# Grouped-query attention of a fused layer step: maxima of two heads in one pair of matmuls, tiles of keys two by two, and other engines for copies and sums

## The chip, the cores and the metric

The kernel runs on one core of a Trainium2 chip. Its metric is the device time of one execution in microseconds (us). The profile gives for the core the busy time of its engines: TensorE (PE, with its weight loads as PEld), VectorE (DVE), ScalarE (ACT), GpSimd (POOL) and the queue of SyncE (SP), which issues most DMAs.

## The reference

One layer of a hybrid backbone for 256 context tokens and 2048 latent tokens: three mixers (differential attention, grouped-query attention, a state-space scan) share an input and an output projection, and a feed-forward layer follows. The change is in the grouped-query attention of the latent tokens. It has four query heads of width 64, two for each of two key heads, and 2560 keys (2048 latent, 512 cached):

```python
qg = q.reshape(b, t, GQA_KV_HEADS, GQA_Q_HEADS // GQA_KV_HEADS, GQA_HD)
s = jnp.einsum('bqkgd,bskd->bkgqs', qb, k).astype(jnp.float32) * scale
p = jax.nn.softmax(s, axis=-1).astype(v.dtype)
return jnp.einsum('bkgqs,bskd->bqkgd', p, v)
```

## The kernel before, in words

The function `attention` (line 842) first does the differential heads, 64 steps and 7 more that drain its pipeline, and then the grouped heads. These are cut into eight units (line 933): a key head `j` and a stretch of 512 queries, both query heads of the group together. Queries and keys are kept as a rounded part in the float32r format and the remainder, in stacks: `qa` holds for each head 64 partitions of the rounded part and 64 of the remainder, `qb[0:64]` the rounded part again, and its partition 64 takes the negated maximum of each query. `gk[j][:, 0]` holds the rounded keys twice, in partitions 0-63 and 64-127; `gk[j][0:65, 1]` their remainder and a row of ones.

A unit has two parts. `maxima` (line 945) finds for each query the maximum over all keys of an approximate score, `qa` times `gk[j][:, 0]`: for each head and each 128 queries five matmuls of 512 keys, each reduced by VectorE out of its bank into `gmx` (lines 959 and 960); then a reduction to `nm` (962), transposes (967) and two copies of a row into `qb` (968). `weighted` (line 971) goes over 20 tiles of 128 keys: four matmuls give the scores of both heads less the maximum (981 and 982, product of two parts each), ScalarE takes the exponential of the two banks at once into `ge` (984), and two tiles later the values are accumulated, the two heads in 64 columns of the array each (990; an f32 matmul is two instructions in the profile). The sum of the exponentials is kept in `ga`, by VectorE for tiles 1 and 3 of every five and by GpSimd for the others (998 and 1000). `unit_tail` (1006) adds the two sums (1009), turns the output (1013), sums over the partitions by matmuls with ones (1020) and divides (1023, 1025).

The order is written out by hand with generators. While `weighted` of unit `ui` runs, each of its 44 steps takes one step of `maxima` of unit `ui + 1`, so that a maximum's matmul stands between scores and values; every second step takes one of the tails, of the attention of the context tokens (`contexts`, units 1 to 3) and of the loads and splits of the output weights (`OutProj.weights`, from unit 4 on, lines 1398 and 1399). Every engine works its instructions in this order. The queries of the next unit are loaded at the start of a unit (`group_queries`, line 936, on SP's queue), into buffers that come free with the last scores of the unit before. The maxima of unit 0 run with wider pieces of 1024 keys (`wide`) in the seven steps that drain the differential heads.

Of the eight PSUM banks the scores have two buffers of two banks (`ps_s`), the single tiles two buffers of one bank (`ps_t`), the outputs two banks.

## Time and profile before

| | |
|---|---|
| three runs, median (range) | 3765.62 us (3758.86 to 3769.51) |
| profiled execution: its own time, its span | 3772.03 us, 3770.2 us |
| TensorE matmuls busy, instructions | 3586.9 us (95%), 20178 |
| VectorE | 2490.2 us (66%), 4092 |
| ScalarE | 1787.6 us (47%), 2890 |
| GpSimd | 1797.8 us (48%), 1448 |

A busy share is a mean over stages with different limits. The matmuls of TensorE overlap and their ends are modelled, so that the distance of two starts says what one costs, and the duration how long its result takes. An idle time is put down to what ended it. Stretches are in us from the start of the span; the grouped heads lie from about 1481 to 1957 us.

### The profile page before, as it was taken

The numbers are of one execution on the slowest core, as the hardware profiler recorded it, in microseconds if no ns is written. First come the engines' busy times: TensorE is split into PE (matmuls) and PEld (weight loads), VectorE is DVE, ScalarE is ACT, GpSimd is POOL, SyncE is SP. The second block draws the span as 40 slices with busy tenths as digits, with TensorE's granted clock in tenths as the row PEclk, the third lists the DMA queues.
The fourth block names the chain that finished last, engine by engine and source line by source line (L and its number), as shares of the span: only waits on it lengthen the run. The fifth ranks groups of instructions, "written<-read, shape, count | busy, mean of one in ns | idle before, by whom it ended". The sixth has DMA issues, their size and how long they took to land.

```text
span 3770.2 us, 53905 instructions
## 1 busy us (share of the span) xinstructions
PE 3586.9 (95%) x20178; PEld 2884.0 (76%) x20178; DVE 2490.2 (66%) x4092; ACT 1787.6 (47%) x2890; POOL 1797.8 (48%) x1448
## 2 busy tenths in 40 slices
PE   6999899988999999999999989999999999999998
PEld 4888699984555555454458879999999999888886
DVE  3666766658889888767746776656556555465476
ACT  3555545546888885444334443334334333333232
POOL 3334356645788886445544567774233232011011
PEclk8999899998999999999999999999999999999999
DMA  5111244345311103001014656665454444645464
GB/s 199 49 46 46 76 126 124 119 130 164 97 34 42 36 22 83 14 26 48 23 62 165 209 190 216 213 216 182 153 186 164 160 154 163 231 160 175 153 217 156
DMA packets 265797, 473.65 MB, mean 126 GB/s; under 512 B 43480, under 2 KB 165752, under 8 KB 260928
## 3 DMA queue, kind: packets, MB, share of 16 engines
q1 hardware_dynamic: 247584, 456.72, 36.7%
q10 hardware_dynamic: 17232, 11.09, 1.1%
q8 instruction: 160, 2.62, 0.3%
q0 software_dynamic: 720, 2.38, 0.2%
q14 instruction: 101, 0.83, 0.1%
HBM read 345.72 MB, written 124.40 MB: 125 GB/s over the span
## 4 chain that ended last, share of the span: by engine, by line
PE 75%; DVE 9%; POOL 6%; issue 4%; DMA 3%; ACT 2%; SPq 0%; POOLq 0%; DVEq 0%; ACTq 0%
PE f L1685 6%; PE f L1684 6%; PE f L1683 6%; PE fy L1960 5%; PE fy L1962 5%; PE fy L1961 5%; PE ps L1174 4%; PE po L1234 4%; PE gpo L990 4%; PE px L225 3%; PE pt L1223 3%; PE gm L959 3%; PE gs L981 2%; PE gs L982 2%; PE opo L1447 2%
## 5 line engine op out<-in xcount | busy, mean ns | idle before, releaser
L1179 DVE TENSOR_SCALAR_CACHE_REDUCE e<-ps 128x1024 f32<-128x1024 f32 (+1 forms) x384 | 392.9, 1040 | 68.5 <-PE ps L1174 67.2
L1190 ACT ACTIVATE e<-e,nb 128x2560 f32<-128x2560 f32 x128 | 311.0, 2430 | 41.0 <-DVE nb L1184 40.9
L1960 PE MATMUL fy<-fp 128*128 128x512 f32 x792 | 308.7, 390 | 0.6 <-DVE fu L1823 0.6
L1962 PE MATMUL fy<-fp 128*128 128x512 f32 x792 | 308.7, 390 | 0.0
L1961 PE MATMUL fy<-fp 128*128 128x512 f32 x792 | 308.4, 389 | 0.0
L1212 POOL TENSOR_TENSOR e<-e,e 128x512 f32<-128x512 f32 x254 | 296.5, 1167 | 21.2
L1924 DVE TENSOR_TENSOR fp<-fo,fp 128x1536 fp32r<-128x1536 f32 (+1 forms) x110 | 208.7, 1911 | 140.5 <-ACT fp L1923 118.0
L960 DVE TENSOR_REDUCE gmx<-gm 128x1 f32<-128x512 f32 (+1 forms) x304 | 214.2, 715 | 120.0 <-PE gm L959 116.8
L1823 POOL TENSOR_TENSOR ft<-fu,fa 128x384 f32<-128x384 f32 x66 | 104.2, 1578 | 390.8 <-DVE fu L1823 342.8
L1991 POOL TENSOR_TENSOR fr<-fr,ln2b 128x1024 f32<-128x1024 f32 x17 | 54.0, 3178 | 490.6 <-DMA fo<-h_d 294.6
L1174 PE MATMUL ps<-dk,dq 96*128 96x512 f32 x640 | 244.9, 466 | 29.8 <-DVE e L1179 18.1
L1000 POOL TENSOR_TENSOR gag<-gag,ge 128x1024 f32<-128x1024 f32 x80 | 208.4, 2605 | 125.7 <-ACT ge L984 124.4
L984 ACT ACTIVATE ge<-gs 128x1024 f32<-128x1024 f32 x160 | 163.7, 1024 | 217.7 <-PE gs L982 215.3
L1923 ACT ACTIVATE fp<-fo 128x1536 fp32r<-128x1536 f32 (+1 forms) x110 | 157.2, 1442 | 195.1 <-PE fy L1962 163.8
L1211 POOL TENSOR_SCALAR e<-e,c 128x512 f32<-128x512 f32 x254 | 180.7, 711 | 115.2 <-DVE c L1203 104.9
L1174 PEld LDWEIGHTS ps<-dk,dq 96*128 96x128 f32 x640 | 101.0, 198 | 156.8 <-issue 72.1
L1224 ACT ACTIVATE wT<-pt 128x512 f32<-128x512 f32 x320 | 178.7, 591 | 67.8 <-PE pt L1223 67.1
L1234 PE MATMUL po<-wT,vl 128*64 128x256 f32 x1280 | 204.5, 407 | 0.0
L1223 PEld LDWEIGHTS pt<-cst,e 128*128 128x128 f32 x1280 | 160.7, 142 | 56.5 <-POOL e L1212 12.5
L1223 PE MATMUL pt<-cst,e 128*128 128x128 f32 x1280 | 197.1, 276 | 4.8 <-POOL e L1212 3.2
L225 PE MATMUL px<-xhTrue,wx 128*128 128x260 f32 (+2 forms) x864 | 182.1, 303 | 16.5 <-DVE l L374 7.0
L1685 PE MATMUL f<-fxt,wc 128*128 128x384 f32 x528 | 179.1, 339 | 2.6 <-DVE wc L1791 2.6
(454 smaller groups left out, 10613.0 us busy)
## 6 DMA issues: line engine op xcount, KB each, us to landing
fo<-in_wfo SPq DMA_DIRECT2D x110, 512.0 KB, 4.2
wq<-in_wfi SPq DMA_DIRECT2D x88, 512.0 KB, 3.7
wq<-ws_d SPq DMA_DIRECT2D x88, 512.0 KB, 4.2
h_d<-h SPq DMA_DIRECT2D x66, 384.0 KB, 3.0
wada<-in_w_ada SPq DMA_DIRECT2D x24, 1024.0 KB, 6.9
ws_d<-wq SPq DMA_DIRECT2D x44, 512.0 KB, 2.6
fo<-h_d SPq DMA_DIRECT2D x66, 256.0 KB, 4.1
fr<-x2T_d SPq DMA_DIRECT2D x20, 768.0 KB, 7.6
```

The source lines that it names most:

```text
L225: PE.matmul(out, l, r, start=(i == 0), stop=(i == n - 1))
L1174: PE.matmul(ps[:, 512 * c:512 * c + 512], Q[0:96, m, qs], K[0:96, m, k0:k0 + 512], start=True, stop=True)
L1179: V.tensor_scalar(self.e[m][:, k0:k0 + w], ps[:, c:c + w], dscale, -3.4e38, ALU.mult, ALU.max, accum_out=mx[:, m, seen[m]:seen[m] + 1])
L1190: S.activation(self.e[m], self.e[m], AF.Exp, bias=self.nb[:, m:m + 1], accum_out=self.l[:, m:m + 1])
L1212: G.tensor_tensor(e0[:, a:b], e0[:, a:b], e1[:, a:b], ALU.add)
L1223: PE.transpose(pt[:, k], self.e[0][:, 128 * (4 * g + k):128 * (4 * g + k) + 128], ident)
L1234: PE.matmul(po[64 * e:64 * e + 64], hd.v[:, k + e], self.wT[:, k + e], start=(k == 0), stop=(k == NKT - 2))
L1683: PE.matmul(o, w[:, 0, c, cs], x[:, 0, k], start=(k == 0), stop=False)
L1685: PE.matmul(o, w[:, 1, c, cs], x[:, 0, k], start=False, stop=(k == 3))
L1960: PE.matmul(o, x[:, 0, ts_], x[:, 0, hs], start=(f == 0), stop=False)
L1961: PE.matmul(o, x[:, 0, ts_], x[:, 1, hs], start=False, stop=False)
L1962: PE.matmul(o, x[:, 1, ts_], x[:, 0, hs], start=False, stop=(f == NF - 1))
```

## The change

The maxima are formed from the rounded parts alone: `qb` gets the second head's rounded part in partitions 64-127, and the matmuls of the two heads go to the two halves of the array's rows, into two banks. Unit 0 uses the wide buffers and one reduction for both heads; the other units take two single banks, VectorE reduces the first, ScalarE copies the second to SBUF and VectorE reduces the copy. `weighted` takes two tiles per turn: scores of two tiles, a step, values of the two tiles before, a step, 21 steps in all; the first two tiles' scores start with the matmuls that don't need the maxima. VectorE keeps the sum of every fourth tile, GpSimd of the others, each addition in two halves of 512 columns; GpSimd also adds the two sums. One row of maxima is copied by ScalarE. Every step takes a step of the side work, the tail has three steps more, the output weights have one buffer (a tag that another tile of the pool used) and three more steps between load and split.

```diff
@@ -940,65 +940,93 @@
                       gp[0].tile([128, 2, 512], F32R, name=f"q{a}{ui}", tag=f"q{a}") for a in "ab"]
             load(qa, stk_d[8 + 2 * j:10 + 2 * j, :, t0:t0 + 512].rearrange("r p t -> p r t"))
             load(qb[0:64], stk_d[8 + 2 * j:10 + 2 * j, 0:64, t0:t0 + 512].rearrange("r p t -> p r t"))
+            load(qb[64:128, 0], stk_d[9 + 2 * j, 0:64, t0:t0 + 512])
             gqs[ui] = qa, qb
 
-        def maxima(ui, wide=False):
+        def maxima(ui, sp=None):
+
+
             j, u = units[ui]
-            qa, qb = gqs[ui]
+            qb = gqs[ui][1]
             nm = nms[ui % 2]
             mx = c1.tile([128, 8, 5], F32, name=f"gmx{ui}", tag="gmx", bufs=2)
-            for r in range(2):
-                for q in range(4):
-                    ql = qa[:, r, 128 * q:128 * q + 128]
-                    pieces = range(0, KEYS, 1024 if wide else 512)
-                    for i, c in enumerate(pieces):
-                        w = min(KEYS - c, pieces.step)
-                        ps = (ps_s if wide else ps_t).tile([128, pieces.step], F32, name=f"gm{ui}_{r}{q}{c}",
-                                                           tag="s" if wide else "t")
-                        for e in range(0, w, 512):
-                            PE.matmul(ps[:, e:e + 512], ql, gk[j][:, 0, c + e:c + e + 512], start=True, stop=True)
-                        V.tensor_reduce(mx[:, 4 * r + q, i:i + 1], ps[:, 0:w], AX.X, ALU.max)
-                        yield
-            V.tensor_reduce(nm[:, :, 64], mx[:, :, 0:len(pieces)], AX.X, ALU.max, negate=True)
+            for q in range(4):
+                for i in range(5):
+                    nm_ = f"gm{ui}_{q}{i}"
+                    if sp is None:
+                        p = ps_s.tile([128, 1024], F32, name=nm_, tag="s").rearrange("p (r t) -> p r t", r=2)
+                        ps = [p[:, r] for r in range(2)]
+                    else:
+                        ps = [ps_t.tile([128, 512], F32, name=f"{nm_}{r}", tag="t") for r in range(2)]
+                    for r in range(2):
+                        hs = slice(64 * r, 64 * r + 64)
+                        PE.matmul(ps[r], qb[hs, 0, 128 * q:128 * q + 128], gk[j][hs, 0, 512 * i:512 * i + 512],
+                                  start=True, stop=True)
+                    if sp is None:
+                        V.tensor_reduce(mx[:, q::4, i], p, AX.X, ALU.max)
+                    else:
+                        cp = sp.tile([128, 512], F32, name=f"{nm_}c", tag="gc", bufs=3)
+                        S.activation(cp, ps[1], AF.Copy)
+                        V.tensor_reduce(mx[:, q, i:i + 1], ps[0], AX.X, ALU.max)
+                        V.tensor_reduce(mx[:, 4 + q, i:i + 1], cp, AX.X, ALU.max)
+                    yield
+            V.tensor_reduce(nm[:, :, 64], mx, AX.X, ALU.max, negate=True)
             yield
             for r in range(2):
                 pt = ps_t.tile([128, 4, 128], F32R, name=f"gpt{ui}_{r}", tag="t")
                 for q in range(4):
                     PE.transpose(pt[0:66, q], nm[:, 4 * r + q], identr)
-                V.tensor_copy(qb[64:65, r], pt[64:65].rearrange("p q t -> p (q t)"))
-                yield
+                row = pt[64:65].rearrange("p q t -> p (q t)")
+                if r:
+                    S.activation(qb[64:65, r], row, AF.Copy)
+                else:
+                    V.tensor_copy(qb[64:65, r], row)
 
         def weighted(ui, sp, ps_o, tails):
             j, u = units[ui]
             qa, qb = gqs.pop(ui)
             po = ps_o.tile([128, 512], F32, name=f"gpo{ui}", tag="o")
             acc, held, es = {}, {}, {}
-            for kt in range(NKT + 2):
-                if kt < NKT:
-                    ks = slice(128 * kt, 128 * kt + 128)
-                    ps = ps_s.tile([128, 1024], F32, name=f"gs{ui}_{kt}", tag="s").rearrange("p (r t) -> p r t", r=2)
+
+            def scores(kts):
+
+                ps = [ps_s.tile([128, 1024], F32, name=f"gs{ui}_{kt}", tag="s").rearrange("p (r t) -> p r t", r=2)
+                      for kt in kts]
+                for kt, p in zip(kts, ps):
                     for r in range(2):
-                        PE.matmul(ps[:, r], gk[j][:, 0, ks], qa[:, r], start=True, stop=False)
-                        PE.matmul(ps[:, r], gk[j][0:65, 1, ks], qb[0:65, r], start=False, stop=True)
-                    e = es[kt] = sp.tile([128, 2, 512], F32, name=f"ge{ui}_{kt}", tag="ge", bufs=5)
-                    S.activation(e, ps, AF.Exp, scale=gscale)
+                        PE.matmul(p[:, r], gk[j][:, 0, 128 * kt:128 * kt + 128], qa[:, r], start=True, stop=False)
+                for kt, p in zip(kts, ps):
+                    for r in range(2):
+                        PE.matmul(p[:, r], gk[j][0:65, 1, 128 * kt:128 * kt + 128], qb[0:65, r],
+                                  start=False, stop=True)
+                    e = es[kt] = sp.tile([128, 2, 512], F32, name=f"ge{ui}_{kt}", tag="ge", bufs=6)
+                    S.activation(e, p, AF.Exp, scale=gscale)
+
+            def values(k):
+                e = es.pop(k)
+                for r in range(2):
+                    PE.matmul(po[64 * r:64 * r + 64, :], gv[j][:, k], e[:, r], start=(k == 0), stop=(k == NKT - 1))
+                eng, nm = (V, "v") if k % 4 == 1 else (G, "g")
+                if nm not in held:
+                    held[nm] = e
+                    return
+                was = acc.get(nm, held[nm])
+                if nm not in acc:
+                    acc[nm] = sp.tile([128, 2, 512], F32, name=f"ga{nm}{ui}", tag=f"ga{nm}")
+                for r in range(2):
+                    eng.tensor_tensor(acc[nm][:, r], was[:, r], e[:, r], ALU.add)
+
+            for kt in range(0, NKT + 2, 2):
+                if kt == 0:
+                    scores((0, 1))
+                elif kt < NKT:
+                    scores((kt,))
+                    scores((kt + 1,))
                 yield
                 if kt >= 2:
-                    k = kt - 2
-                    e = es.pop(k)
-                    for r in range(2):
-                        PE.matmul(po[64 * r:64 * r + 64, :], gv[j][:, k], e[:, r],
-                                  start=(k == 0), stop=(k == NKT - 1))
-                    eng, nm = (V, "v") if k % 5 in (1, 3) else (G, "g")
-                    if nm not in acc:
-                        if nm not in held:
-                            held[nm] = e
-                        else:
-                            acc[nm] = sp.tile([128, 2, 512], F32, name=f"ga{nm}{ui}", tag=f"ga{nm}")
-                            eng.tensor_tensor(acc[nm], held[nm], e, ALU.add)
-                    else:
-                        eng.tensor_tensor(acc[nm], acc[nm], e, ALU.add)
-                yield
+                    values(kt - 2)
+                    values(kt - 1)
+                    yield
             oT = sp.tile([128, 512], F32, name=f"goT{ui}", tag="goT")
             S.activation(oT, po, AF.Copy)
             tails.append(unit_tail(ui, sp, ps_o, acc, oT))
@@ -1006,18 +1034,20 @@
         def unit_tail(ui, sp, ps_o, acc, oT):
             j, u = units[ui]
             yield
-            V.tensor_tensor(acc["v"], acc["v"], acc["g"], ALU.add)
+            for r in range(2):
+                G.tensor_tensor(acc["g"][:, r], acc["g"][:, r], acc["v"][:, r], ALU.add)
             yield
             px = ps_o.tile([128, 4, 128], F32, name=f"gpx{ui}", tag="x")
             for q in range(4):
                 PE.transpose(px[:, q], oT[:, 128 * q:128 * q + 128], ident)
             o = sp.tile([128, 4, 2, 64], F32, name=f"go{ui}", tag="go")
             S.activation(o, px.rearrange("p q (r d) -> p q r d", d=64), AF.Copy)
-            yield
+            for _ in range(4):
+                yield
             pl = ps_o.tile([128, 4, 2, 2], F32, name=f"gpl{ui}", tag="x")
             for r in range(2):
                 for q in range(4):
-                    PE.matmul(pl[:, q, r], acc["v"][:, r, 128 * q:128 * q + 128], ones2, start=True, stop=True)
+                    PE.matmul(pl[:, q, r], acc["g"][:, r, 128 * q:128 * q + 128], ones2, start=True, stop=True)
             yield
             rl = sp.tile([128, 4, 2], F32, name=f"grl{ui}", tag="grl")
             V.reciprocal(rl, pl[:, :, :, 0])
@@ -1317,7 +1347,7 @@
                 if step == 3 * n + 1:
                     gk.append(group_keys(0))
                     group_queries(0)
-                    first = maxima(0, True)
+                    first = maxima(0)
             run(first)
 
         group_values = lambda j: load_v(256 + 64 * j, I["cgv"][:, 64 * j:64 * j + 64], CTX, KEYS, f"vg{j}")
@@ -1332,19 +1362,18 @@
             more = iter(())
             if ui + 1 < len(units):
                 group_queries(ui + 1)
-                more = maxima(ui + 1)
+                more = maxima(ui + 1, gsp)
             if ui == 1:
                 gv.append(group_values(1))
                 gk.append(group_keys(1))
-            for i, _ in enumerate(weighted(ui, gsp, ps_o, tails)):
+            for _ in weighted(ui, gsp, ps_o, tails):
                 next(more, None)
-                if i % 2:
-                    if tails and next(tails[0], run) is run:
-                        tails.pop(0)
-                    if 1 <= ui < 4:
-                        next(ctx, None)
-                    if ui >= 4:
-                        next(wo, None)
+                if tails and next(tails[0], run) is run:
+                    tails.pop(0)
+                if 1 <= ui < 4:
+                    next(ctx, None)
+                if ui >= 4:
+                    next(wo, None)
             run(more)
             if ui == 3:
                 run(ctx)
@@ -1392,9 +1421,10 @@
     def weights(self, pool):
         nc = self.tc.nc
         for k in range(8):
-            raw = pool.tile([128, 1024], F32, name=f"wor{k}", tag="wor")
+            raw = pool.tile([128, 1024], F32, name=f"wor{k}", tag="osq", bufs=1)
             nc.sync.dma_start(out=raw, in_=self.I["w_out"][128 * k:128 * k + 128, :])
-            yield
+            for _ in range(4):
+                yield
             nc.scalar.activation(self.wh[:, k], raw, AF.Copy)
             nc.vector.tensor_tensor(self.wl[:, k], raw, self.wh[:, k], ALU.subtract)
             yield
```

## Rows read from the trace of the kernel before

**Rows 1.** stages: us, busy us (xcount) per engine, TensorE clock, DMA share, GB/s
```profile
1440.00:1481.00 41.00, 39.95 (x241) 22.18 (x237) 33.66 (x43) 18.33 (x29) 18.58 (x20) 1.00 0.25 55
1804.00:1860.00 56.00, 55.32 (x229) 27.80 (x228) 38.86 (x52) 21.68 (x22) 29.63 (x12) 1.00 0.07 19
1916.00:1957.00 41.00, 40.80 (x168) 17.64 (x164) 11.24 (x8) 18.90 (x20) 27.41 (x12) 1.00 0.10 33
```
**Rows 2.** the chain of waits from 1400 to 2000 us, by line
```profile
by line: PE gpo L990 22.4%; PE gm L959 16.3%; PE gs L981 11.8%; PE gs L982 11.6%; DVE gmx L960 4.0%; PE po L1234 3.6%; DVE gav L1000 3.2%; PE pt L1223 2.3%; PE ps L1174 2.0%; PE gpl L1020 2.0%; issue 1.8%; DVE wol L1399 1.6%; DMA lncol<-in_
```
**Rows 3.** timeline of one tile: start us, us, engine, line, operation
```profile
1820.45 0.50 PE L959 MATMUL gm<-gk,qa 128*128 128x512 f32 x1
...
1820.79 0.39 PE L981 MATMUL gs<-qa,gk 128*128 128x512 f32 x1
...
1821.50 0.40 PE L982 MATMUL gs<-qb,gk 65*128 65x512 f32 x1
...
1821.73 0.39 PE L959 MATMUL gm<-gk,qa 128*128 128x512 f32 x1
...
1821.93 1.03 ACT L984 ACTIVATE ge<-gs 128x1024 f32<-128x1024 f32 x1 [1.58 <-PE gs L982]
...
1822.05 1.08 PE L990 MATMUL gpo<-ge,vg 128*64 128x512 f32 x4
...
1823.06 0.50 PE L959 MATMUL gm<-gk,qa 128*128 128x512 f32 x1
```
**Rows 4.** timeline at the end of the last unit: three tiles of values together
```profile
1954.00 2.79 PE L990 MATMUL gpo<-ge,vg 128*64 128x512 f32 x12
```
**Rows 5.** groups by line, 1541 to 1957 us: busy us, mean ns, idle before
```profile
L960 DVE TENSOR_REDUCE gmx<-gm 128x1 f32<-128x512 f32 x236 | 160.0, 687 | 100.1 <-PE gm L959 97.7
...
L984 ACT ACTIVATE ge<-gs 128x1024 f32<-128x1024 f32 x138 | 141.2, 1024 | 187.5 <-PE gs L982 185.1 <-PE gm L959 1.9 <-ACT woh L1398 0.6
...
L1000 POOL TENSOR_TENSOR gag<-gag,ge 128x1024 f32<-128x1024 f32 x70 | 182.2, 2604 | 113.4 <-ACT ge L984 112.3
...
L1000 DVE TENSOR_TENSOR gav<-gav,ge 128x1024 f32<-128x1024 f32 x42 | 63.0, 1499 | 22.2 <-ACT ge L984 22.2
...
L1003 ACT ACTIVATE goT<-gpo 128x512 f32<-128x512 f32 x7 | 4.2, 598 | 18.8 <-PE gpo L990 18.8
```
**Rows 6.** timeline, and line 719 in 0.05 us: matmuls of 64 partitions
```profile
1630.92 0.38 PE L1071 MATMUL psc<-ckq,cqa 64*128 64x256 f32 x1
...
1631.23 0.38 PE L1070 MATMUL psc<-ckq,cqa 128*128 128x256 f32 x1
...
495.30:495.35 0.05, 0.03 (x2) 0.04 (x2) 1.00 0.37 123
```
**Rows 7.** timeline where units 5 and 6 begin their values
```profile
1804.18 1.08 PE L990 MATMUL gpo<-ge,vg 128*64 128x512 f32 x4
...
1860.37 1.08 PE L990 MATMUL gpo<-ge,vg 128*64 128x512 f32 x4
```
**Rows 8.** timeline: VectorE and GpSimd adding; then line 1000, ns min/median/max
```profile
106.43 1.22 POOL L491 TENSOR_TENSOR dx<-xt,d_bc 128x512 f32<-128x512 f32 x1
...
107.20 0.74 DVE L518 TENSOR_TENSOR E<-E,E 128x256 f32<-128x256 f32 x1
...
107.73 1.35 POOL L492 TENSOR_TENSOR y<-y,dx 128x512 f32<-128x512 f32 x1
...
107.86 1.51 DVE L498 TENSOR_TENSOR M<-E,Gt 128x256 f32<-128x256 f32 x1
...
L1000 DVE TENSOR_TENSOR gav<-gav,ge x42: 1209/1251/2952, 1569.2 to 1953.0; 128x1024 f32<-128x1024 f32 x42
```
**Rows 9.** timeline of GpSimd, stage before: one addition of 512 columns
```profile
1005.34 1.28 POOL L1212 TENSOR_TENSOR e<-e,e 128x512 f32<-128x512 f32 x1
```
**Rows 10.** timeline: a VectorE reduction out of SBUF while GpSimd adds
```profile
1486.74 2.42 POOL L998 TENSOR_TENSOR gag<-ge,ge 128x1024 f32<-128x1024 f32 x1 [0.87 <-ACT ge L984]
...
1487.92 1.21 DVE L920 TENSOR_REDUCE ossl<-osql 128x16 f32<-128x1024 f32 x1
```

## The prediction

> **What bounds the kernel now.** I read the page's busy shares first, then the stages, the chain of waits, and a timeline of one tile. Over the span TensorE is busy 95%, but that is a mean over many stages; the change touches one of them, the grouped heads, from about 1481 to 1957 us, with a lead-in from 1444. There TensorE is busy 55.3 of 56.0 us, VectorE 38.9, GpSimd 29.6 (53%) and ScalarE 21.7 [rows 1]. The chain of waits of this stretch is mostly TensorE's four groups of matmuls (values, maxima, two scores); VectorE's maxima hold 4.0% and its additions 3.2% [rows 2]. So TensorE sets the pace, and a saving there counts until another queue holds it up.
>
> One tile of keys takes 2.61 us, from one maximum behind the values to the next, 1820.45 to 1823.06 [rows 3]: 0.34 us from this maximum to the first score, 0.71 over three steps to the last score (0.235 each), 0.23 to the second maximum, 0.32 to the values, 1.01 for the values. Values without a break cost 0.43 us for a head pair's half: 12 of them last 2.79 us where 4 last 1.08, so (2.79-1.08)/4 for each two more [rows 3, 4]. A tile's values alone would be 0.86. Going from the full array to 64 columns and back therefore costs (0.32-0.235)+(1.01-0.86)+(0.34-0.235) = 0.34 us, once per tile.
>
> **The change, part by part.** *Paired maxima.* A unit has 40 maxima matmuls now; the change makes 20 pairs, the heads in partitions 0-63 and 64-127. Two such matmuls do start together: in line 719, which carries states in the same two halves of the partitions (in plain f32), two starts fall into 0.05 us [rows 6]. A short matmul of 64 partitions between full ones takes 0.31 us to the next start, for 256 columns [rows 6]; 512 columns stream in 0.235, so these 256 in 0.12, and the change of shape adds 0.19. I price a pair at 0.235+0.19 = 0.42 us.
>
> *Two tiles at a time.* Between two values blocks lie now eight scores, and a pair before and behind the values. Per two tiles: scores 8 x 0.235 + 0.19 = 2.07; two pairs 0.85; values 4 x 0.43 + 0.15 = 1.87. Sum 4.79 us against 2 x 2.61 = 5.22, so 0.43 less, 4.3 us per unit of 20 tiles. Where shapes change from 64 partitions straight to 64 columns, no row shows it: below, nothing beyond these prices; above, two drained matmuls (under the rivals). I take the first, since both changes seen cost about the same.
>
> By the Trainium skill, "TensorEngine Tiling (Array Packing)", section Key Properties, a change of the tiling mode drains TensorE. The rows' 0.34 and 0.19 contain whatever drains there is; the rule makes a rival out of the change no row shows.
>
> *Ends of a unit.* The last pair has no scores ahead of it; it needs both banks, and ScalarE's copy of the pair before takes 0.60 [rows 5] after a matmul of 0.50 [rows 3], so it waits 0.50+0.60-0.32 = 0.8 us. I add 0.4 for the opening, where four tiles' scores and two pairs stand ahead of the first values and exponentials of 1.02 [rows 5] free the banks. The second maxima row on ScalarE lies beside the opening's four scores that don't need it (0.94 us); uncovered it would be 0.6 per unit. Net 4.3-1.2 = 3.1 us for each of seven units that carry maxima: **-21.7 us**. The last unit has none and saves one round trip per two tiles: 10 x 0.34 = **-3.4 us**.
>
> *The lead-in.* Unit 0's maxima run in the stage where TensorE is busy 39.95 of 41 us [rows 1]. At best 20 matmuls go, 20 x 0.235 = 4.7; at worst 20 pairs add as many changes of 0.19, 3.8. VectorE has 20 reductions of 1024 instead of 16 and 8 halves, the same work. I take **-1.5 us**, range -4.7 to +2.
>
> *ScalarE's copies.* 20 per unit at 0.60 [rows 5]: 12 us more on 21.7 busy of 56 [rows 1]. Walked from a pair of tiles' first score: the fourth score starts at 0.81, its exponential 0.43 later, as 1821.50 to 1821.93 shows [rows 3], at 1.24; the second ends at 3.28, the copy at 3.88. The next pair of maxima comes at 2.07+0.42+1.87 = 4.36. Hidden by the values; without that slack each copy would cost up to 0.6.
>
> *VectorE.* Still 40 reductions of 0.69 [rows 5], half of them out of SBUF. That GpSimd's additions do not hold these up is seen once: 1024 columns took 1.21 while GpSimd was adding [rows 10], the rate of a lone one. Its additions fall from seven per unit to four (the first tile of each engine is only held), and the sum of totals leaves it, 1.2 us as the least of line 1000 [rows 8]. By busy time, per two tiles VectorE has 4 x 0.69 and 0.5 of additions, 3.3 us, ScalarE 2 x 1.02 + 2 x 0.60 = 3.2, both below 4.79: what can stop TensorE is not their load but the order of their queues.
>
> *GpSimd and the halves.* An addition with two SBUF operands waits for the other engine's whole instruction. On VectorE 256 columns took 0.74 and then 1.51 us, because GpSimd's first addition ended at 107.65 and its next ran from 107.73 to 109.08, between VectorE's two [rows 8]. So a VectorE addition in two halves can wait twice. GpSimd goes from 11 additions and 2.60 each [rows 5] to 14 and the sum, each in two halves of 1.28 [rows 9]: 15 x 2.56 + 1 = 39 us of about 53, 74% where it was 53%. The halves fit, but they are running just where VectorE's addition stands: right behind the two exponentials.
>
> On the walk VectorE's addition comes at 4.6, behind the reduction of the copy, and undisturbed ends at 5.8. The next bank, from the pair at 4.36, is read behind it, until 6.5; TensorE's next pair wants it at 4.79+2.07 = 6.86. Slack 0.35. Queued behind the addition: two reductions, and behind them the pair and the values. Below: no stall. Above: both halves wait, 0.64 on average and a whole 1.28, less 0.35: 1.55 us. Near rows: VectorE's additions average 1.50 against a least of 1.21 [rows 5, 8], 0.29 of waiting at 53%; at 74% and for two pieces 0.29 x 1.4 x 2 = 0.81, less 0.35: 0.5 us. Four in each of seven units: 28 x 0.5 = **+14 us**.
>
> *The rest.* One more load of 128 KB per unit goes onto SP's queue behind two of the same unit, asked for when the buffers come free a whole unit boundary ahead of use: nothing; uncovered, its landing time, some microseconds once per unit. Output weights in one buffer with four steps between load and split: nothing, since a step is over 2 us; uncovered, a landing for each of eight. Six exponential buffers for five: needed for the pairs.
>
> **Sum**: -21.7 - 3.4 - 1.5 + 14 = -12.6 us. The profiled execution took 3772.0 us, so 3759.4 for it; it lies 6.4 above the median of the three runs, so I forecast 3753.0.
>
> **Rivals.** *TensorE's saving comes through whole*: GpSimd's halves miss VectorE's additions. For: mean waits are short today, most VectorE additions last near their least [rows 8]. Against: the order of the queues puts both behind the same exponentials. Then -26.6: 3739, down to 3730 if the pairs change shape more cheaply.
>
> *VectorE held up by GpSimd turns the sign.* Both halves wait each time, 1.55 x 28 = 43 us, TensorE's pairs waiting on VectorE's reductions. -26.6+43 = +17: 3782. It decides slower from 1.35 us per addition (28 x 1.35 = 26.6+11.3). For: the alternation in [rows 8]. Against: GpSimd is not busy throughout, and waits on exponentials [rows 5].
>
> *A pair costs TensorE more than its price.* Either the two don't run side by side (140 x 0.235 = 33 us more, less the 14 of additions that then find slack), 3772; or the direct change of shape drains: a matmul's 0.39 duration against 0.235 [rows 3], 0.155 twice per two tiles, 70 x 0.31 = 22: 3775. For: that change isn't in the trace. Against: [rows 6] has starts together. By the skill's rule on drains named above this would be the outcome; no run here shows it.
>
> **How the numbers follow.** Forecast 3753, its own range 3743 to 3763: chance 0.48. Whole saving 3739: 0.25. Sign turned, 3777 to 3790: 0.15. Dear pairs, 3772 to 3775: 0.12. A measurement can tell some 0.3%, 11.3 us: below 3754.3 is faster, above 3776.9 slower. Faster takes the whole saving and half of the forecast's case, 0.50; same the other half and the dear pairs, 0.35; slower 0.15. The range 3732 to 3778 leaves out the lowest of the second case and most of the third.
>
> **What would show it.** The distance between two units' first values, 56.2 us now (1804.18 to 1860.37 [rows 7]), should be near 55: 53 if the saving is whole, 58 if the sign turns. Two values blocks should lie 4.8 us apart, except every second time, where VectorE's addition stands; its halves should last over 0.64 where GpSimd is adding. Two maxima matmuls should start within 0.02 us. If the pairs' starts lie 0.2 apart, if TensorE waits for ScalarE's copies, or GpSimd fills the units, I am wrong about which queue holds the saving back.

## The result, and the profile after

The changed kernel takes 3792.6 us (median of 4 runs, 3792.5 to 3806.7) against 3762.2 (4 runs): 1.0088 times as long, 95% interval 1.0059 to 1.0116. It is slower, and outside the predicted range of 3732 to 3778. The profiled execution is one of 3792.62 us, span 3790.8.

From the first to the last values of the grouped heads it is 506.2 us instead of 470.4. Ahead of the lead-in the profiled execution is 13 us ahead of that of before, through stages that the change doesn't touch (the profiled execution of before lies 9.8 above its median); the lead-in, from the first maxima (1430.9, before 1444.1) to the first values, is 40.7 us instead of 41.7, and the rest behind the last values 1.0 shorter. So the loss lies in these 36 us. Stages of after (columns as in [rows 1]; first the grouped heads; then 60 us of them, to set beside [rows 1]) and the same stretch of before:

```profile
1471.60:1977.80 506.20, 458.97 (x1864) 225.48 (x1864) 313.49 (x453) 270.59 (x401) 341.23 (x251) 0.92 0.11 31
1840.00:1900.00 60.00, 52.75 (x197) 25.09 (x197) 36.39 (x46) 28.79 (x38) 37.23 (x28) 0.84 0.08 25
```
```profile
1485.80:1956.20 470.40, 455.16 (x1867) 226.13 (x1867) 319.62 (x457) 199.45 (x256) 245.00 (x104) 0.98 0.11 33
```

TensorE is busy about as long as before (459.0 and 455.2 us) though it has less to do, because the mean granted clock is 0.92 instead of 0.98, and it stands idle for 47.2 us instead of 15.2. In the chain of waits (after, 1400 to 2000 us; compare [rows 2]) VectorE's additions now hold 9.4% where they held 3.2:

```profile
by line: PE gpo L1008 18.4%; PE gs L997 10.1%; DVE gav L1017 9.4%; PE gm L963 8.2%; PE gs L1000 7.9%; issue 6.8%; ACT ge L1003 5.0%; PE po L1264 2.7%; PE gpl L1050 2.7%; DVE gmx L970 2.7%; DVE gmx L971 2.4%; POOL gag L1017 2.3%; PE pt L1253
```

Groups of lines of after, 1481 to 1977 us (compare [rows 5]), and its waits (us, times, longest):

```profile
L1017 POOL TENSOR_TENSOR gag<-gag,ge 128x512 f32<-128x512 f32 x203 | 283.1, 1426 | 87.3 <-ACT ge L1003 87.3
...
L1003 ACT ACTIVATE ge<-gs 128x1024 f32<-128x1024 f32 x154 | 150.4, 1021 | 73.0 <-PE gs L1000 69.2 <-POOL gag L1017 2.0 <-PE gm L963 1.8
...
L970 DVE TENSOR_REDUCE gmx<-gm 128x1 f32<-128x512 f32 x135 | 92.6, 686 | 100.7 <-PE gm L963 100.4
...
L1017 DVE TENSOR_TENSOR gav<-gav,ge 128x512 f32<-128x512 f32 x48 | 67.4, 1442 | 15.2 <-ACT ge L1003 15.2
```
```profile
PE gm L963 <- DVE gmx L970: 23.2, 18, 2.7
...
PE gm L963 <- ACT gm_33c L969: 3.6, 5, 0.7
```

A VectorE half lasts 1.44 us, more than a whole addition's least of 1.21 [rows 8]. TensorE waits for the reduction of the first bank (L970) for 23.2 us, for ScalarE's copies hardly. The reductions themselves take 0.69 as before. The timeline of after shows one such stop, and later two blocks of values with nothing in the way:

```profile
1845.12 9.34 POOL L1017 TENSOR_TENSOR gag<-gag,ge 128x512 f32<-128x512 f32 x6 [1.01 <-ACT ge L1003]
...
1847.03 0.50 PE L963 MATMUL gm<-gk,qb 64*128 64x512 f32 x2
1847.36 1.38 DVE L1429 TENSOR_TENSOR wol<-wor,woh 128x1024 fp32r<-128x1024 f32 x1 [0.25 <-ACT woh L1428]
...
1848.66 3.44 DVE L1017 TENSOR_TENSOR gav<-gav,ge 128x512 f32<-128x512 f32 x2
...
1849.53 0.50 PE L963 MATMUL gm<-gk,qb 64*128 64x512 f32 x1
1852.03 0.68 DVE L970 TENSOR_REDUCE gmx<-gm 128x1 f32<-128x512 f32 x1
...
1852.76 0.49 PE L963 MATMUL gm<-gk,qb 64*128 64x512 f32 x1 [2.73 <-DVE gmx L970]
1853.18 3.46 PE L1008 MATMUL gpo<-ge,vg 128*64 128x512 f32 x8
...
1909.63 1.94 PE L1008 MATMUL gpo<-ge,vg 128*64 128x512 f32 x8
1911.50 0.50 PE L963 MATMUL gm<-gk,qb 64*128 64x512 f32 x2
...
1914.42 1.94 PE L1008 MATMUL gpo<-ge,vg 128*64 128x512 f32 x8
```

GpSimd adds six halves in a row. VectorE's two halves, of which the shortest of this run took 0.68 us, take 3.44 between them, behind a split of the output weights of 1.38. So the first bank of the pair at 1847.03 is read only at 1852.03. The next pair's first matmul (1849.53) doesn't wait for this reduction, its second waits 2.73 for it, and the next eight values take 3.46 us instead of 1.94, since the granted clock has fallen (0.54 over these 3.46 us). Where nothing stops them, two blocks of values lie 4.79 us apart (1909.63 to 1914.42), what the prediction's sum gives. The period was right; what comes between was not.

### The profile page after: what moved, and what is told of

It is laid out like the page before. It is cut to its first block, busy times and chain, and to the rows that moved or that the text cites. A ratio compares the mean times of both kernels' runs of the same rounds, so it can differ in the third digit from the quotient of the medians.

```text
span 3790.8 us, 54322 instructions
## 1 busy us (share of the span) xinstructions
PE 3574.7 (94%) x20178; PEld 2870.6 (76%) x20178; DVE 2476.3 (65%) x4080; ACT 1859.6 (49%) x3038; POOL 1900.7 (50%) x1600
## 4 chain that ended last, share of the span: by engine, by line
PE 72%; DVE 10%; POOL 7%; issue 4%; ACT 4%; DMA 3%; SPq 0%; POOLq 0%; ACTq 0%; DVEq 0%
PE f L1715 6%; PE f L1714 6%; PE f L1713 6%; PE fy L1990 5%; PE fy L1992 5%; PE fy L1991 5%; PE ps L1204 4%; PE po L1264 4%; PE px L225 3%; PE gpo L1008 3%; PE pt L1253 3%; PE opo L1477 2%; PE opo L1476 2%; PE opo L1475 2%; PE gs L997 2%
## 5 line engine op out<-in xcount | busy, mean ns | idle before, releaser
L1017 POOL TENSOR_TENSOR gag<-gag,ge 128x512 f32<-128x512 f32 x208 | 289.3, 1423 | 87.3 <-ACT ge L1003 87.3
L1715 PE MATMUL f<-fxt,wc 128*128 128x384 f32 x528 | 179.0, 339 | 2.6 <-DVE wc L1821 2.6
L1714 PE MATMUL f<-fxt,wc 128*128 128x384 f32 x528 | 178.8, 339 | 1.7 <-DVE fxt L1647 1.7
```

What stands on the lines that cost most here:

```text
L1714: PE.matmul(o, w[:, 0, c, cs], x[:, 1, k], start=False, stop=False)
L1715: PE.matmul(o, w[:, 1, c, cs], x[:, 0, k], start=False, stop=(k == 3))
```

## The experiments

Theory: VectorE's halves wait for GpSimd's, TensorE's pairs wait for VectorE, and the clock falls behind the stops. Rivals: the pairs or the order of two tiles let the clock fall, ScalarE's copies hold the banks, GpSimd is the bound. This table has, for each run, the distance from first to last values, in it TensorE's busy time, the rest (idle) and the mean granted clock, all from the row of that stretch in one profiled execution, and the time of the kernel (a median where several runs are given). Executions of one kernel lie up to 28 us apart (e9, 3774.0 to 3801.6), and how much the stretch alone varies was not measured, so a difference of a few us between two rows needs a second sign. The kernel before, run again beside each group of experiments, had medians of 3760.5 to 3766.3; the ratios below are to those.

| run | first to last values | busy | idle | clock | kernel, us (runs) |
|---|---|---|---|---|---|
| before | 470.4 | 455.2 | 15.2 | 0.98 | 3762.2 (4) |
| after | 506.2 | 459.0 | 47.2 | 0.92 | 3792.6 (4) |
| e1 no VectorE additions | 457.1 | 433.0 | 24.1 | 0.95 | 3742.7 |
| e2 no additions | 447.5 | 427.5 | 20.0 | 0.97 | 3735.6 |
| e3 both whole | 478.7 | 445.3 | 33.4 | 0.94 | 3770.7 |
| e4 all on GpSimd | 523.8 | 455.6 | 68.2 | 0.89 | 3818.6 |
| e5 VectorE whole, GpSimd halves | 491.2 | 454.4 | 36.8 | 0.92 | 3784.6 |
| e6 VectorE halves, GpSimd whole | 553.2 | 484.8 | 68.4 | 0.86 | 3844.4 |
| e7 halves apart | 488.0 | 440.8 | 47.2 | 0.94 | 3783.6 |
| e8 no copy | 525.0 | 470.3 | 54.7 | 0.89 | 3818.1 |
| e9 whole, old split | 490.9 | 448.4 | 42.5 | 0.94 | 3792.0 (6) |
| e10 whole, even split | 470.1 | 439.5 | 30.6 | 0.96 | 3763.1 (12) |
| e11 before, halves | 479.1 | 457.5 | 21.6 | 0.98 | 3764.0 |
| e12 before, no additions | 446.9 | 446.3 | 0.6 | 0.99 | 3731.5 |
| e13 e10, full maxima | 477.6 | 440.5 | 37.1 | 0.96 | 3767.6 |
| e14 e10, own bank | 464.1 | 436.8 | 27.3 | 0.96 | 3759.5 (8) |
| e15 e2, contexts apart | 466.0 | 441.2 | 24.8 | 0.91 | 3757.0 |
| e16 e12, contexts apart | 476.5 | 460.7 | 15.8 | 0.95 | 3767.3 |
| e17 before, even split | 477.8 | 462.4 | 15.4 | 0.96 | 3759.1 (12) |
| e18 e14, totals apart | 460.5 | 431.3 | 29.2 | 0.98 | 3753.7 (11) |

**e1 and e2: additions left out**, in e1 VectorE's, in e2 for all `k` but 0 and 2. The sum of totals and the division by the sums are left out too (a constant instead); only the first place of e1's edit is shown.

```diff
-                eng, nm = (V, "v") if k % 4 == 1 else (G, "g")
+                if k % 4 == 1:
+                    return
+                eng, nm = G, "g"
```


> Leaves out VectorE's additions (every fourth tile is not summed), the sum of totals, and the division by the sums (by a constant instead); everything else as in the changed kernel. Theory: VectorE's halves alternate with GpSimd's, so TensorE's next pair waits for VectorE's bank, and these stops let the granted clock fall. Then with no VectorE additions the saving is whole: units about 53 us apart, first to last values of the grouped heads 440 to 455 us where the kernel before has 470 and the changed one 506, half-clock time between 1430 and 1990 us at most 35 us (92 changed, 24 before), whole kernel 3735 to 3750. Rival (the paired 64-partition matmuls or the order of two tiles lower the clock, or ScalarE's copies stop TensorE): first to last values stays above 485, half-clock time above 60, whole kernel above 3775.

> Leaves out all additions of exponentials but one of GpSimd's per unit, the sum of totals, and the division by the sums. Theory (alternation of VectorE and GpSimd is the only harm): the same as without VectorE's additions, within 6 us. Rival (GpSimd's 30% more work stops something by itself, by the exponentials' buffers that it frees or by VectorE's other operations): over 10 us faster than without VectorE's additions alone.

e1 falls to 457.1, 2 us past its range, and far from the rival's 485. At half clock TensorE still spends 48 us between 1430 and 1990 us, where the theory allowed 35 (after: 92): not all falls of the clock stand behind VectorE's additions. VectorE's additions cost 49.1 us: 23.1 of them idle TensorE, 26.0 longer busy time at the lower clock (0.92 for 0.95). e2 is 9.6 below e1, between its two expectations: that much GpSimd's own additions cost. The pairs, the order and ScalarE's copies are all still there at a clock of 0.97: they alone don't bring it down to 0.92. As the main cause the rival falls.

**e3, e5, e6: whole or in halves, four ways.** The edit is one operation of 1024 columns for the two of 512, on both engines (e3, the sum of totals too), on VectorE (e5) or on GpSimd (e6):

```diff
-                for r in range(2):
-                    eng.tensor_tensor(acc[nm][:, r], was[:, r], e[:, r], ALU.add)
+                eng.tensor_tensor(acc[nm], was, e, ALU.add)
```


> Additions of both engines, and the sum of totals, as one operation of 1024 columns instead of two of 512; all else as in the changed kernel. Theory: a VectorE addition then waits once, for up to a whole GpSimd addition of 2.6, where two halves wait twice for up to 1.28 each: if both halves nearly always wait, a mean wait of 1.3 against 1.6 and the stage is 5 to 25 us shorter than 506; whole kernel 3765 to 3788. Rival (it isn't the splitting but that GpSimd is adding whenever VectorE's addition stands): 500 to 515 us, no change.

> Only VectorE's additions become one operation of 1024 columns; GpSimd's stay in halves. First to last values of the grouped heads was 506 us in the changed kernel, 479 with both whole, 457 without VectorE's. Theory (each VectorE addition waits for one whole GpSimd operation, and halves wait twice): it waits once and for at most 1.28, so 460 to 474 us. Rival (VectorE gets in only when GpSimd pauses, however GpSimd's work is cut): as with both whole or worse, 476 to 500 us.

> Only GpSimd's additions become one operation of 1024 columns; VectorE's stay in halves. Theory (each VectorE half waits for one whole GpSimd operation): both halves may wait for 2.4 instead of 1.28, 510 to 560 us from first to last values. Rival (the cost lies in VectorE's two pieces, not in what they wait for): 500 to 512 us.

The halves alone cost 27.5 us (506.2 to 478.7), a little more than the 5 to 25 expected. e6 hits the theory: two VectorE halves take 5.62 us beside three whole GpSimd additions that take 8.48, 2.8 each, so that each half waits for about a whole one. Timeline of e6:

```profile
1894.12 8.48 POOL L1020 TENSOR_TENSOR gag<-gag,ge 128x1024 f32<-128x1024 f32 x3 [5.19 <-ACT ge L1003]
...
1897.53 5.62 DVE L1018 TENSOR_TENSOR gav<-gav,ge 128x512 f32<-128x512 f32 x2
...
1903.81 0.79 PE L963 MATMUL gm<-gk,qb 64*128 64x512 f32 x1 [4.79 <-DVE gmx L970]
```

e5 contradicts the theory as I had put it: it should have been best and is worse than e3 (491.2, the rival's range). Its timeline shows why a wait isn't bounded by one GpSimd operation:

```profile
1503.23 13.65 POOL L1018 TENSOR_TENSOR gag<-gag,ge 128x512 f32<-128x512 f32 x11
...
1509.85 8.12 DVE L1020 TENSOR_TENSOR gav<-gav,ge 128x1024 f32<-128x1024 f32 x1
```

VectorE's addition, 1.21 alone, ends at 1517.97, 1.1 us after GpSimd's chain of halves ended (1516.88): it got in when the chain was over. In the stop at 1848.66 above it got in within a chain. Both happen; what decides which, no run here shows.

**e4: all additions on GpSimd** (`eng, nm = G, "g"`, and no sum of totals).

> GpSimd does all additions (19 per unit, in halves), VectorE none and there is no sum of totals; all else as in the changed kernel. Theory: no alternation, TensorE runs without VectorE's waits; GpSimd has 19 x 2.56 = 48.6 us per unit, just below the 53 that TensorE needs: first to last values 445 to 465, half-clock time under 40, whole kernel 3738 to 3760. Rival (GpSimd becomes the bound through the exponentials' buffers, or the pairs lower the clock): above 485 us.

The theory fails by 59 us. The time is in the rival's range, but not by its way: TensorE waits for VectorE's reductions, hardly for exponentials. What holds VectorE are its other operations on SBUF: groups of e4 (split of the weights, two SBUF inputs, 1.82 us each before; the sign of the context maxima, one input, 0.45 each before), its waits, and its timeline:

```profile
L1427 DVE TENSOR_TENSOR wol<-wor,woh 128x1024 fp32r<-128x1024 f32 x8 | 45.1, 5638 | 2.1 <-ACT woh L1426 2.1
...
L1104 DVE TENSOR_SCALAR mxc<-mxc 128x4 f32<-128x4 f32 x6 | 19.9, 3324 | 0.2
```
```profile
PE gm L963 <- DVE gmx L970: 50.4, 12, 9.3
PE gs L997 <- ACT ge L1003: 4.8, 9, 1.2
```
```profile
1527.43 2.53 POOL L1017 TENSOR_TENSOR gag<-ge,ge 128x512 f32<-128x512 f32 x2
...
1527.67 12.10 DVE L1104 TENSOR_SCALAR mxc<-mxc 128x4 f32<-128x4 f32 x1
...
1529.92 9.82 POOL L1017 TENSOR_TENSOR gag<-gag,ge 128x512 f32<-128x512 f32 x8
```

Four elements per partition took 12.1 us, until ten halves in a row (1527.43 to 1539.74) were through. Units 0 and 3, with no such operation in them, were as short as in e1. By the Trainium skill, "SBUF — State Buffer", section "SBUF: two separate sides", GpSimd and a VectorE instruction that has two SBUF inputs, or runs in a mode that uses both ports, share a pair of ports, and whichever starts first holds it for its whole instruction. e6 agrees, with its two waits of about a GpSimd addition; e4 and e5 show more than it says, in e4 a wait of ten GpSimd instructions in a row.

**e7: the second half behind the next pair's reductions** (the last of three places of the edit).

```diff
                     values(kt - 1)
+                    if late:
+                        late.pop(0)()
                     yield
+                    if late:
+                        late.pop(0)()
```


> VectorE's two halves are no longer issued together: the first stays behind the values, the second goes behind the next pair's two reductions. Same operations. Theory (TensorE's next pair waits because two waiting halves stand ahead of the bank's read): one half of 1.4 mean fits beside two reductions in the 2.4 us of a pair, so 460 to 480 us from first to last values, granted clock over the stretch 0.94 or more. Rival (any wait of VectorE stops the pairs, together or apart): 500 us or more.

Between the two: 488.0, clock 0.94. Taking the halves apart gives back 18 of 49 us.

**e8: no copy.** ScalarE's copy is left out, VectorE reduces `ps[1]` itself.

> ScalarE's copy of the second head's bank is left out; VectorE reduces both banks itself, as many columns as before. Theory (VectorE's queue is what TensorE waits for): the second bank too now waits for VectorE, 505 to 530 us from first to last values, whole kernel 3790 to 3815. Rival (ScalarE's copies hold the banks): below 500 us.

525.0, as the theory has it (the kernel, 3818.1, lies 3 above its range): ScalarE's copies help.

**e9, e10: other splits, additions and sum of totals whole** (`k % 5 in (1, 3)` and `k % 2` for VectorE).

> Paired maxima and two tiles at a time as in the changed kernel, but additions whole (1024 columns) and split as in the kernel before (VectorE takes tiles 1 and 3 of every 5, so 7 additions for it and 11 for GpSimd per unit, instead of 4 and 14); sum of totals whole on GpSimd. Theory (VectorE waits for a busy GpSimd, and TensorE's stops and the lower clock behind them are the loss): GpSimd has 11 x 2.4 = 26 us of 53, pauses in every two tiles, so VectorE's additions last near 1.5 and fit beside four reductions (4.3 of 4.79 us); 452 to 470 us from first to last values, whole kernel 3742 to 3758, faster than the kernel before by 0.1 to 0.5%. Rival (each VectorE addition behind the reductions costs TensorE a stop, whatever GpSimd does): 7 in place of 4, so more than the 479 of both whole, and slower than before.

> As the one with the old split, but VectorE adds every odd tile and GpSimd every even one (9 each per unit). Theory: GpSimd has 9 x 2.4 = 22 us of 53, one addition per two tiles, so no chain of them; VectorE has 4 x 0.69 + 1.55 = 4.3 us in every period of 4.79, little slack; 450 to 472 us, whole kernel 3740 to 3760. Rival (VectorE's load now stops TensorE): 475 to 500 us.

The old split is the rival's case: 490.9, ratio to before 1.007 (1.0043 to 1.0097). Two of its ten pairs of tiles have both additions on GpSimd, and the chain stands before VectorE's next one; that this is the cause is argued, not shown. With one addition per engine and pair of tiles it is 470.1, in the theory's range, but the kernel, 3763.1, lies 3 above it: as fast as before, ratio 0.9997 (0.9985 to 1.0009). e10's timeline: GpSimd pauses over 3 us between its additions:

```profile
1832.79 2.37 POOL L1016 TENSOR_TENSOR gag<-gag,ge 128x1024 f32<-128x1024 f32 x1 [2.42 <-ACT ge L1003]
1838.44 2.38 POOL L1016 TENSOR_TENSOR gag<-gag,ge 128x1024 f32<-128x1024 f32 x1 [3.28 <-ACT ge L1003]
```

**e11, e17: one edit on the kernel before**, halves (e11) or `k % 2` (e17).

> The kernel before with one edit: the additions of both engines in two halves of 512 columns. First to last values 470 us before. Theory (halves on both engines make VectorE wait twice, and TensorE stops behind it): seven additions per unit wait longer, 485 to 520 us, granted clock below 0.96 over the stretch. Rival (halves hurt only with the new order of two tiles and its busier GpSimd): 466 to 476 us.

> The kernel before with one edit: VectorE adds every odd tile and GpSimd every even one (9 each per unit instead of 7 and 11). Theory (an addition of VectorE is dear where GpSimd is in a chain of its own): GpSimd has one addition of 2.6 per 5.2 us and always pauses between, 460 to 468 us from first to last values where 470 stand, 3752 to 3760 for the whole. Rival (two more additions on VectorE, each behind the maxima, cost more than the pauses give): 470 to 482 us, slower than before by up to 0.3%.

With halves the stretch is 8.7 us longer there, between the two expectations; the kernel's time, 3764.0 beside 3762.7, doesn't show it. The even split: the kernel, 3759.1, is in the theory's range, ratio 0.9986 (0.9974 to 0.9999); the 477.8 is in the rival's, but from the slowest of 12 executions. Which of the two holds is open.

**e12: before, no additions** (the same operations left out as in e2).

> The kernel before without additions, just as in the run of the changed kernel without additions: all but one of GpSimd's per unit, the sum of totals and the division by the sums are left out. Theory (the saving of pairs and two tiles at a time is there, 25 us): 465 to 470 us from first to last values (470 with additions, 447.5 for the changed kernel without), since VectorE's additions cost the kernel before little. Rival (the kernel before loses as much to its additions, and the true saving is smaller): 450 to 462 us.

The surprise of the study. Stages of e2 and e12, first to last values:

```profile
1476.00:1923.50 447.50, 427.45 (x1866) 213.50 (x1864) 220.74 (x389) 269.16 (x401) 37.88 (x31) 0.97 0.12 34
```
```profile
1472.40:1919.30 446.90, 446.26 (x1866) 224.52 (x1867) 224.60 (x394) 199.35 (x256) 37.15 (x24) 0.99 0.12 34
```

Without additions both orders take the same time. TensorE is busy 18.8 us less in the new one, and is idle 20.0 where the old one is idle 0.6. Additions cost the kernel before 23.5 us, the changed one 58.7. Distances of first values by unit, and the last unit:

| | 0 | 1 | 2 | 3 | 4 | 5 | 6 | 7 |
|---|---|---|---|---|---|---|---|---|
| e2 | 50.2 | 73.7 | 73.1 | 51.7 | 53.0 | 56.2 | 51.3 | 38.3 |
| e12 | 53.5 | 63.6 | 68.1 | 56.7 | 55.0 | 55.1 | 54.1 | 40.9 |

Units 1 and 2, in which the context heads' matmuls lie, lose 15.1 us; the other six gain 14.6. In these two units together TensorE is idle 12.0 us in e2 and 0.4 in e12, and busy 3.4 longer, at a clock of 0.93 where e12 has 0.99. e2's longest waits there:

```profile
PE ptc L1128 <- DVE gmx L970: 4.7, 6, 0.8
PE gs L997 <- ACT ge L1003: 2.7, 4, 1.1
PE ptc L1128 <- ACT gm_22c L969: 1.4, 2, 0.7
```

L1128 are the context heads' transposes: they wait until a pair's banks are read.

**e13: full maxima.** `qa[:, r]` and `gk[j][:, 0]` again for the pair's operands, in e10.

> The kernel with an even split of whole additions, its maxima again as two matmuls over the full 128 partitions instead of a pair over 64 each; order of two tiles, ScalarE's copy and additions as they are. Two matmuls of 0.235 for a pair priced at 0.42: 0.05 more per pair, 140 pairs, +7 us on 470 if the price is right (475 to 481). Rival (pairs cost TensorE as much as two matmuls or more, by their changes of shape or a lower clock): 460 to 471 us. If pairs ran at half of two matmuls, 0.235, without a change of shape: 495 to 505.

477.6 is in the range that the price gives, but not by that way: TensorE's busy time rose by 1.0 us only, its idle time by 6.5. Two undisturbed blocks of values lie 4.84 us apart in e13, 4.79 in e10: the pairs as such save 0.05 per two tiles, half of what I had.

**e14: the context transposes in the outputs' bank**, in e10.

```diff
-                        pt = ps_t.tile([128, 4, 128], F32, name=f"pt{nm}{qt}{g}", tag="t")
+                        pt = ps_x.tile([128, 4, 128], F32, name=f"pt{nm}{qt}{g}", tag="x")
```


> The kernel with an even split of whole additions; the transposes of the context heads take the bank of the outputs instead of one of the two that the pairs use. Units 1 and 2 last 149.4 us together there, 147.4 without additions, 142.8 before. Theory (these units lose because a transpose there waits for a bank that holds a pair, and the next pair for the transpose's copy): 138 to 145 us for the two, whole kernel 3752 to 3759, 0.1 to 0.3% faster than before. Rival (they lose for VectorE's longer queue or the contexts' own matmuls): 147 to 152 us, whole kernel as before.

Unit 1 falls from 76.2 to 71.7 us, unit 2 stays (72.6, 72.2): 143.9 together (e10 148.8), in the theory's range, but a third of the 15 us at most. The transposes' waits for the pairs, 4.7 and 1.4 us in e10 as in e2, are gone. Ratio to before 0.9982 (0.9970 to 0.9994); the interval overlaps that of e10, so the kernel's time alone doesn't show the gain.

**e15, e16: context heads apart**, no additions: `next(ctx, None)` taken out, so that all their steps run behind unit 3.

> The changed kernel without additions (as e2: no additions but one, constant in place of the sums), and the context heads no longer mixed into units 1 to 3: all of their steps run by themselves behind unit 3. Theory (the prediction's saving of 3.1 us per unit is there in plain units, and what takes it away is the mixing with the context heads): units 1, 2 and 3 last 49.5 to 52.5 us each, 2.5 to 4 less than in the same edit of the kernel before. Rival (units 1 and 2 are long for another reason, their loads or their place): over 60 us each, as in e2 (74.3 and 73.1).

> The kernel before without additions (as e12), context heads run by themselves behind unit 3. Both theories: units 1, 2 and 3 last 52.5 to 56 us each.

Units 0, 1 and 2 take 49.5, 54.8, 54.8 us in e15 and 52.8, 55.1, 55.0 in e16. Over the whole stretch e15 is 10.5 us shorter than e16 (466.0, 476.5), where e2 and e12 differ by 0.6: the mixing takes away 11 us of the saving. But units 1 and 2 are not down to 52.5, between the two expectations (unit 3 can't be read, since the context heads now follow in it; e2's unit 1 is 73.7, not the 74.3 of the expectation). Units 0 and 1 of e15, then the same of e16:

```profile
1479.60:1529.10 49.50, 48.49 (x210) 23.29 (x208) 29.83 (x48) 31.88 (x45) 7.34 (x6) 1.00 0.32 85
1529.10:1583.90 54.80, 53.80 (x230) 26.38 (x228) 28.16 (x43) 32.08 (x44) 3.56 (x4) 0.94 0.08 22
```
```profile
1478.90:1531.70 52.80, 52.79 (x211) 25.71 (x210) 30.58 (x49) 21.38 (x24) 7.30 (x5) 1.00 0.35 93
1531.70:1586.80 55.10, 55.10 (x231) 27.87 (x232) 29.03 (x44) 21.71 (x23) 3.47 (x2) 1.00 0.07 20
```

A later unit has 20 short matmuls more than unit 0 (tails of the one before), 2.3 us in e16. The other 3 us of e15's unit 1 are the clock. Its timeline and its stretches of 4 us show where:

```profile
1541.45 1.95 PE L1050 MATMUL gpl<-cst,gag 128*128 128x2 f32 x16
...
1544.74 1.02 PE L1000 MATMUL gs<-qb,gk 65*128 65x512 f32 x2
...
1546.41 3.68 PE L1008 MATMUL gpo<-ge,vg 128*64 128x512 f32 x8
```
```profile
1541.00:1545.00 4.00, 4.00 (x27) 3.47 (x26) 1.44 (x3) 1.13 (x2) 0.00 (x0) 0.97 0.00 0
1545.00:1549.00 4.00, 4.00 (x10) 1.09 (x11) 1.45 (x3) 2.01 (x3) 0.76 (x1) 0.50 0.00 0
1549.00:1553.00 4.00, 4.00 (x14) 2.04 (x10) 1.35 (x2) 1.24 (x2) 0.29 (x1) 0.68 0.22 66
```

Behind the 16 two-column matmuls of the totals the granted clock falls from 1.00 to 0.50 (from 2.4 to 1.2 GHz) for about 7 us, though TensorE is not idle. So it does in units 2, 3 and 5 of e15, for half as long in 7, not in 4 and 6. In e16, with the same 16 matmuls, it does so once, for half as long. What makes the difference is open.

**e18: the totals in two groups**, in e14.

```diff
                     PE.matmul(pl[:, q, r], acc["g"][:, r, 128 * q:128 * q + 128], ones2, start=True, stop=True)
-            yield
+                yield
```


> The kernel of e14 (even split of whole additions, context transposes in the bank of the outputs) with one more edit: the 16 two-column matmuls of a unit's totals go in two groups, one step of the loop apart, instead of all at once. Theory (16 short matmuls in one piece let the clock fall, about 3 us each time in the units that follow): the falls at the totals are gone or shorter, first to last values 452 to 460 us where e14 has 464, whole kernel 3745 to 3756, 0.3 to 0.6% faster than the kernel before. Rival (the clock falls for the stops and the context heads around them, not for these matmuls): 461 to 468 us, ratio to the kernel before as that of e14, 0.998.

460.5, half a microsecond past the theory's range and out of the rival's; the clock over the stretch rises from 0.96 to 0.98, TensorE's busy time falls by 5.5. Behind the totals the clock is at 0.50 for 27 us in e14 (four falls) and for 7 in e18 (one); elsewhere for 7 and 14. So in these two profiles the totals set off part of the falls. Ratio to the kernel before 0.9971 (0.9960 to 0.9981), 3753.7 us against 3764.4: **this version is 0.3% faster than the kernel before.** That it is faster than e14 is not shown by the kernels' times, since the intervals overlap.

## Why the prediction was wrong

*What bounds the kernel* was right as far as it went: TensorE sets the pace and the order of VectorE's queue stops it. *Two tiles at a time* and *pairs* were right per period: 4.79 us, pairs start together (x2 in 0.50 us), a direct change of shape drains nothing beyond the prices. So the rival of dear pairs falls. By the Trainium skill, "TensorEngine Tiling (Array Packing)", section Key Properties, a change of the tiling mode drains TensorE; beyond the 0.19 and 0.34 us of the rows no cost of it shows here. *Ends of a unit*: 1.0 us idle in e15's unit 0, for 1.2. *Lead-in*: -1.0 for -1.5 (how the range's end of +2 follows from the 3.8 named there is not said). *ScalarE's copies* are nearly hidden (3.6 us of waits in after, and VectorE in their place costs more, e8), *VectorE's reductions* out of SBUF not held up (0.69).

Two steps failed. From first to last values the sum had -25.1 + 14 = -11.1 us, and +35.8 came. **First, the price of VectorE's addition in halves**: +14 us, from 0.5 us of stop each. Net of what the additions cost the kernel before it was 58.7 - 23.5 = +35.2. The stop itself was mis-sized: 23.1 us of idle TensorE (after against e1) over 28 additions is 0.8, still within my bound of 1.55. What had no term at all is that TensorE's clock falls behind such stops: 26.0 us, as much again, so that an addition cost 1.75 in all. I had the mechanism as a rival, "VectorE held up by GpSimd turns the sign", and gave it 0.15 and 3790 at most, because I priced stops as stops.

**Second, the saving of 25.1 us**, taken for all units alike. In e2 against e12 it is nothing in sum. It is there in units 0 and 3 to 7, 14.6 us together where the sum had 18.9, and 3.3 for unit 0 where I had 3.1; in the two units with context heads, where it had 6.2, a loss of 15.1 stands instead. The sum has no term for these heads and never asked which banks their transposes use: the pair now takes both. e14 shows this for 4.9 us (units 1 and 2 together, against e10), and e15 against e16 that the mixing takes 11 us of the saving. The rest goes with the lower clock, part of it behind the totals; how much each has is open.

The signs that I had named held where they could: units of the changed kernel lie 58.7 to 67.2 us apart from unit 3 on, beyond the 58 of the turned sign, and halves last 1.44.

## What to carry to other kernels

Price a stop of TensorE twice, as idle time and as the matmuls behind it at the lower clock; here the second was as large as the first. Splitting an addition on VectorE or GpSimd didn't make the other's wait shorter here, where both had a queue: the best split tried gave each engine one whole operation per period, with pauses on GpSimd. Before counting a saving per loop turn, take the turns that carry side work by themselves, with the banks that this work needs.

## What was not expected of the hardware

A VectorE operation of four elements per partition on SBUF lasted 12.1 us behind a GpSimd chain of ten halves (e4). And the granted clock fell to 0.50 without TensorE being idle, behind 16 matmuls of two columns that took 1.95 us (e15); not behind each such group.
